# Gathered rows and activations of the experts transposed in 32x32 blocks on VectorE

## The chip, the cores and the metric

The kernel runs on one core of a Trainium2 chip, as one program. The metric is the device time in microseconds (us) of one execution, lower is better. In the rows PE is TensorE's matmuls and PEld its weight loads, DVE is VectorE, ACT is ScalarE, POOL is GpSimd, and SP is the engine that only issues the loads from memory.

## The reference

One transformer layer over 512 tokens of width 1024: attention and Fourier mixing first, then a mixture of experts, which is where the change lies. All of it is in float32.

```python
def moe(h, ...):                          # h: 512 tokens x 1024
    logits = h @ w_router + b_router
    top_logit, top_idx = lax.top_k(logits, 4)      # 4 of 32 experts for each token
    gates = jax.nn.softmax(top_logit, axis=-1)
    ...                                   # tokens sorted by expert, xb: the tokens of expert e
    g = jnp.minimum(xb @ w_gate[e] + b_gate[e], 7.0)
    u = jnp.clip(xb @ w_up[e] + b_up[e], -7.0, 7.0)
    act = g * jax.nn.sigmoid(1.702 * g) * (u + 1)
    y = act @ w_down[e] + b_down[e]       # 1024 x 1024 weights, three for each expert
    ...                                   # y times gate, added up by token
```

## The kernel before

**Units and kinds.** An expert is one unit of work, 32 in all. Their order is by the number of tokens that chose them, and the place in that order gives each unit a kind, which fixes how many token slots it has: `h` 128 slots (4 units), `m` 96 (13 units, two of them the experts 0 and 1 that come first), `l` 64 (10) and `t` 32 (5). After the first two units they go in 15 pairs, an `m` or `h` with an `l` or `t`: ten pairs m+l, four h+t (the 4th, 8th, 12th and 15th) and, first of all, one m+t. Within a pair the three matrices (`g` gate, `u` up, `d` down) alternate: m g, l g, m u, l u, m d, l d.

**Weights.** A matrix is 1024 x 1024 float32 and comes as four pieces of 1024 KB (`load_piece`, line 978, issued by SP) into a ring of 11 slots. A piece holds two of the eight blocks of 128 input features (k). SP issues a piece as soon as the products of the piece 11 places earlier have left its slot, so SP waits for PE there.

**Products.** `step_mm` makes the products of one k: the activations are the stationary operand and the weights move. PE's columns are used in tiles of 32 or 64 so that several products of few tokens run beside each other: for `m` twelve products of 32 tokens x 256 outputs for each k, for `l` two of 64 x 512, for `t` four of 32 x 256. A float32 product is two matmul instructions in the trace. `h` goes another way: weights and activations are each split into two float32r numbers, and VectorE makes the small part of the weights (`wsplit`, one 128x1024 subtraction for each k).

**Rows in, rows out.** For the product g the stationary operand must have input features on the partitions. The normalised tokens stand in a DRAM buffer (`hx2_d`, written by `post_h`, line 1141) and a unit's tokens are gathered from it: `places` and `table` (DVE) make one-hot rows, `gather` (line 1289) turns them into indices by four small products 128x4, and an indirect DMA (line 1302, POOL) brings the rows, tokens on partitions. `x_trans` (line 1328) then turns them: PE transposes of 128x128 into a PSUM bank, four to a group (two for `t`), and an ACT copy out of PSUM. The activation between u and d (`glu_g`, `glu_u`) has tokens on partitions too, and `a_trans` (line 1441) turns it in the same way. The first unit's x is not turned: `pick` makes it otherwise.

**What sets the order.** It is written out by hand: `emit_mat` emits the eight k of a matrix, and after each k `side_step` runs one step (up to the next `yield`) of at most two waiting side tasks. So `x_trans`, `a_trans`, the fetch of later units (`fetch_of`) and the scatter are spread between the products, one step for each k. `x_of(u+2)` is begun in unit u's matrix d and needed at matrix g of unit u+2, `fetch_of(u+4)` follows it. For unit 1 things are closer: its gather is in matrix g of unit 0, its `x_trans` in matrix u of unit 0, and matrix g of unit 1 is next. Engines run their instructions in order.

Of the kernel before, what the change touches and what calls it, by code (L numbers as in the profile page):

```python
# [36 lines left out]
D = 1024  # L37
# [125 lines left out]
def dit_block(ctx: ExitStack, tc: tile.TileContext, x, c, cctx, c_ctx, w_mod, b_mod, n_ap, n_ao, n_fp, n_fo,  # L163
# [712 lines left out]
    def chain(*gs):  # L876
        for g in gs:
            yield from g
# [262 lines left out]
    def post_h(t):  # L1141

        h, b = (hx[t] if t < 2 else hw[t - 2]).f, s2.f[:, 4 * t + 1:4 * t + 2]
        z = V.scalar_tensor_tensor(h, xr[t].f, b, PRE2, op0=OP.mult, op1=OP.mult)
        if t > 1:
            tc.keep_in_program_order(z)
# [61 lines left out]
    free(vec[0], wr, *hx, *xr[:2], S1f, zb, eq)  # L1208
    more_ring(2)
    xTh, xTl = R(8, 128), R(8, 128)  # L1210
    xTm = alias(xTh, 8, 128)
# [101 lines left out]
    def fetch_of(u):  # L1313

        while fetching:
            yield
        fetching.append(u)
        places(u)
        yield
        table(u)  # L1320
        for _ in range(3):
            yield
        g = gather(u, kinds[u])
        next(g)
        fetching.remove(u)
        yield

    def x_trans(kind, xh, xl=None):
        for half in range(2 if kind in "hm" else 1):
            b = tbank()  # L1330
            n = 2 if kind == "t" else 4
            for k in range(n):
                c = (4 * half + k) * 128
                tr(ps[:, b, k * 128:k * 128 + 128], xg[kind][:, c:c + 128])
            src = ps[:, b, 0:n * 128].rearrange("p (k n) -> p k n", k=n)
            c4 = slice(4 * half, 4 * half + 4)
            if kind == "h":
                split_late(xh.r[:, c4], xl.r[:, c4], src)
            else:
                z = xh[:, 4 * half:4 * half + n]  # L1340
                later(lambda src=src, z=z: act(z, src, AF.Copy), [z], [src], age=0)
            yield

    def back(u, kind):
# [95 lines left out]

    def a_trans(kind):
        a = glu_tiles(kind)[1]
        for half in range(2 if kind in "hm" else 1):
            b = tbank()
            n = min(4, WIDTH[kind] // 128 - 4 * half)
            for k in range(n):
                c = (4 * half + k) * 128
                tr(ps[:, b, k * 128:k * 128 + 128], a[:, c:c + 128])
            src = ps[:, b, 0:n * 128].rearrange("p (k n) -> p k n", k=n)
            c4 = slice(4 * half, 4 * half + 4)  # L1450
            if kind == "h":
                split_late(aTh.r[:, c4], aTl.r[:, c4], src)
            else:
                z = (aTm if kind == "m" else aTf.f)[:, 4 * half:4 * half + n]
                later(lambda src=src, z=z: act(z, src, AF.Copy), [z], [src], age=0)
            yield

    def glu_g(kind, b):
        t_, u_ = glu_tiles(kind)
# [78 lines left out]
    def step_mm(kind, mat, b, k, w, hi, lo, sel, xs):  # L1538

        first = k == 0  # L1540
        if kind == "h":
# [6 lines left out]
            for st, mv, last in ((xh, hi, False), (xh, lo, False), (xl, hi, k == 7)):  # L1548
                for h in range(2):
                    mm(ps[:, b + h], st.r[:, k], mv.r[:, h * 512:h * 512 + 512], start=first, stop=last)  # L1550
                first = False
        elif kind == "m":
# [8 lines left out]
            both = ps[96:128, b].rearrange("p (r n) -> p r n", r=2)  # L1561
            if first:
                bias = biasP.b[0:96, MAT.get(mat, 0)]
                if mat != "d":
                    for p in range(3):
                        mm(out_(0, p, 2), sel.to_broadcast([96, 32]), bias[:, 0:512], start=True, stop=False)
                else:
                    sel = selb.b[0:96, NS + 2:NS + 3]
                mm(both, sel.to_broadcast([96, 32]), bias[:, None, 768:D].to_broadcast([96, 2, 256]), start=True,
                   stop=False)  # L1570
                if mat != "d":
                    for p in range(4):
                        q = unit(2, p)[1]
                        mm(out_(2, p), sel.to_broadcast([96, 32]), bias[:, q * 256:q * 256 + 256], start=True, stop=False)
            for r in range(3):
                for p in range(4):
                    g, q = unit(r, p)
                    n = 1
                    if mat != "d":
                        st = xs[:, k, 32 * g:32 * g + 32]  # L1580
                    else:
                        fq, c = k // 2, k % 2
                        st = xs[:, 2 * fq + c, 32 * g:32 * g + 32] if fq < 3 else xs[:, 2 * g + c, 96:128]
                        if first and p < 3 and r < 2:
                            if r:
                                continue
                            n = 2
                    mm(out_(r, p, n), st, w[:, q * 256:q * 256 + 256 * n],
                       start=first and mat == "d" and (p < 3 or r == 2), stop=k == 7 and r > 0)
        else:  # L1590
            v, n = (64, 512) if kind == "l" else (32, 256)
            a, c = k // (n // 128), k % (n // 128)
            st = xs[:, c, v * a:v * a + v]
            if first and mat != "d":
                for h in range(128 // v):
                    mm(ps[v * h:v * h + v, b, 0:n], sel.to_broadcast([96, v]),
                       biasP.b[0:96, MAT[mat], h * n:h * n + n], start=True, stop=False)
                first = False
            for h in range(128 // v):
                mm(ps[v * h:v * h + v, b, 0:n], st, w[:, h * n:h * n + n], start=first, stop=k == 7)  # L1600

    def sel_of(u):
        kind, e, r = units[u]
# [69 lines left out]
    for i, (u, m) in enumerate(order):  # L1673
        kind = kinds[u]
        if i:
# [2 lines left out]
            if was == "g":  # L1678
                add(glu_g(pk, pb), True)
            elif was == "u":  # L1680
                acted[pu] = add(chain(glu_u(pk, pb, {"h": 2, "m": 2, "l": 3, "t": 5}[kind]), a_trans(pk)), True)
            else:
                finish(summed)
                y_out(pu, pk, pb)
# [36 lines left out]
        elif i == 1:  # L1721
# [5 lines left out]
            aTm = alias(aTh, 6, 128)  # L1727
            yh, yl = R(D), R(D)
            acc = [W(D) for _ in range(4)]

# [3 lines left out]
        elif i == 4:  # L1734
            settle()
            free(xT1)
            bd, gT, g3 = R(D), R(512), W(4, 96)
            xTf = W(4, 128)
        elif i == 6:
            while side and side[0] is not ready[3]:  # L1740
                finish(side.pop(0))
            settle()
            free(bd, g3, gT)
            aTf, u1l, yz = W(4, 128), W(512), R(D)

    while side:
        finish(side.pop(0))
# [136 lines left out]
```

## Time and profile before

| what | value |
|---|---|
| three timed runs | 1412.1, 1416.8, 1417.2 us, median 1416.8 |
| profiled execution, own time | 1413.2 us |
| its span, first to last instruction | 1411.4 us |
| PE busy | 1345.5 us, 95% of the span |
| DVE busy | 719.9 us, 51% |
| ACT busy | 409.3 us, 29% |
| bytes moved by DMA | 468.86 MB, mean 332 GB/s |

The first 340 us are attention and routing, the experts' products go from there to about 1387 us, and 24 us of sums and output follow. Busy time of PE says only that some matmul was under way: its instructions overlap, and their ends are modelled. Distances between the starts of following rows say more.

### The profile page before, as it was taken

To read this page: it belongs to the slowest core of one execution; us is meant where nothing else is said; L and a number is where in the kernel's file an instruction comes from. 1 tells how busy PE (TensorE), PEld (TensorE's weight loads), DVE (VectorE), ACT (ScalarE), POOL (GpSimd) and SP (SyncE) were. 2 spreads that over 40 slices of the span, in tenths; PEclk is the share of its full clock that TensorE was granted. 3 is DMA by queue.
4 is the path that set the end of the run, shared out by engine and by line. 5 is a ranking of instruction groups with operands and counts; after the bars stand their busy time and mean duration, and the time that the engine had idled before them with its cause. 6 is when DMAs were issued, how large, how long until landed. Compare 5 with 4: busy or idle time off the path is not lost. (4 is left out here: it accounts for less than half of the span.)

```text
span 1411.4 us, 30490 instructions
## 1 busy us (share of the span) xinstructions
PE 1345.5 (95%) x12966; PEld 798.2 (57%) x12967; DVE 719.9 (51%) x1329; ACT 409.3 (29%) x634; POOL 121.8 (9%) x90
## 2 busy tenths in 40 slices
PE   5998999998999999999999999999999999999993
PEld 3766887877554545466444454654544466444572
DVE  4676777755452424268423335762324287232575
ACT  5565455632110101035110103421111154010352
POOL 4355000013000000000000000000000000000002
PEclk8999999999998999999999999999999999999997
DMA  9865003667887999999999999999999999999993
GB/s 343 306 229 189 1 0 106 216 228 313 315 295 298 408 397 408 379 409 392 405 409 379 409 374 409 396 408 406 393 384 385 401 395 408 402 408 375 408 380 122
DMA packets 126496, 468.86 MB, mean 332 GB/s; under 512 B 10976, under 2 KB 12316, under 8 KB 126356
## 3 DMA queue, kind: packets, MB, share of 16 engines
q1 hardware_dynamic: 121540, 454.44, 83.2%
q0 software_dynamic: 4816, 12.43, 2.3%
q8 instruction: 103, 1.69, 0.5%
q14 instruction: 37, 0.30, 0.1%
HBM read 464.05 MB, written 6.31 MB: 333 GB/s over the span
## 5 line engine op out<-in xcount | busy, mean ns | idle before, releaser
L266 PE MATMUL ps<-s,s 128*32 128x256 f32 (+11 forms) x5364 | 892.4, 417 | 28.7 <-DMA s<-in_w_mod_dram 8.4
L266 PEld LDWEIGHTS ps<-s,s 128*128 128x128 f32 (+4 forms) x5033 | 510.8, 155 | 315.2 <-issue 182.2
L266 PE MATMUL ps<-s,a 128*32 128x256 f32 (+1 forms) x7026 | 412.7, 383 | 0.0
L266 PEld LDWEIGHTS ps<-s,a 128*32 128x32 f32 x7026 | 216.7, 110 | 158.5 <-issue 18.9
L274 ACT ACTIVATE s<-s 128x1024 fp32r<-128x1024 f32 (+8 forms) x196 | 175.9, 927 | 361.7 <-DVE s L283 308.4
L278 DVE TENSOR_TENSOR s<-s,s 128x1024 fp32r<-128x1024 f32 (+11 forms) x316 | 208.4, 686 | 32.3 <-ACT s L274 28.6
L274 ACT ACTIVATE s<-ps 128x512 fp32r<-128x512 f32 (+5 forms) x168 | 91.3, 553 | 246.0 <-PE ps L266 127.1
L278 DVE TENSOR_TENSOR s<-s,ps 128x512 f32<-128x512 f32 (+1 forms) x129 | 86.5, 682 | 82.1 <-PE ps L266 81.7
L285 DVE TENSOR_SCALAR s<-ps 128x768 f32<-128x768 f32 (+3 forms) x32 | 26.3, 823 | 185.1 <-PE ps L266 185.1
L270 PE MATMUL ps<-s,s 128*128 128x128 f32 x575 | 96.6, 288 | 15.3 <-DVE s L283 9.9
L1302 POOL DMA_INDIRECT s<-hx_d,s x31 | 32.4, 1045 | 893.3 <-PE ps L266 613.2
L270 PEld LDWEIGHTS ps<-s,s 128*128 128x128 f32 x575 | 66.4, 143 | 73.7 <-issue 45.8
L293 DVE COPY s<-ps 128x4 f32<-128x4 f32 (+5 forms) x66 | 23.7, 359 | 141.0 <-PE ps L266 117.0
L274 ACT ACTIVATE a<-ps 128x512 f32<-128x512 f32 (+1 forms) x48 | 25.9, 540 | 219.0 <-PE ps L270 219.0
L278 POOL TENSOR_TENSOR s<-s,s 128x1024 f32<-128x1024 f32 (+1 forms) x23 | 53.7, 2339 | 272.9 <-DVE s L278 211.4
L289 DVE SCALAR_TENSOR_TENSOR s<-ps,s,s 32x256 fp32r<-32x256 f32 (+5 forms) x64 | 46.2, 721 | 58.0 <-ACT s L274 52.0
L274 ACT ACTIVATE s<-ps,s 32x256 fp32r<-32x256 f32 (+7 forms) x68 | 44.8, 669 | 97.9 <-PE ps L266 90.5
L297 DVE TENSOR_TENSOR s<-ps,s 128x512 fp32r<-128x512 f32 (+1 forms) x92 | 60.6, 667 | 22.9 <-ACT s L274 22.8
L283 DVE TENSOR_SCALAR s<-ps 128x768 f32<-128x768 f32 (+4 forms) x33 | 26.5, 803 | 77.6 <-PE ps L266 77.5
L274 ACT ACTIVATE s<-s,s 128x1 f32<-128x1 f32 (+4 forms) x70 | 43.2, 644 | 13.8 <-DVE s L289 7.7
L297 DVE TENSOR_TENSOR s<-s,s 128x192 fp32r<-128x192 f32 (+5 forms) x32 | 36.0, 1144 | 8.5 <-ACT s L274 8.5
L289 DVE SCALAR_TENSOR_TENSOR s<-s,s,s 128x512 fp32r<-128x512 f32 (+5 forms) x48 | 36.8, 796 | 5.9 <-ACT s L274 4.6
(77 smaller groups left out, 289.4 us busy)
## 6 DMA issues: line engine op xcount, KB each, us to landing
s<-in_w_gate_dram SPq DMA_DIRECT2D x128, 1024.0 KB, 10.9
s<-in_w_up_dram SPq DMA_DIRECT2D x128, 1024.0 KB, 10.8
s<-in_w_down_dram SPq DMA_DIRECT2D x128, 1024.0 KB, 7.9
s<-in_w_mod_dram SPq DMA_DIRECT2D x32, 512.0 KB, 4.6
s<-in_w_mod_dram SPq DMA_DIRECT2D x8, 1024.0 KB, 16.3
s<-in_x_dram SPq DMA_DIRECT2D x8, 512.0 KB, 8.3
s<-in_w_out_dram SPq DMA_DIRECT2D x8, 512.0 KB, 5.1
s<-in_w_in_dram SPq DMA_DIRECT2D x1, 2560.0 KB
```

Of the source, the lines that this page charges most:

```text
L266: pin(nc.tensor.matmul(o, a, b, start=start, stop=stop))
L270: pin(nc.tensor.transpose(o, i, ident))
L274: return nc.scalar.activation(o, i, f, **kw)
L278: return eng.tensor_tensor(o, a, b, op=op)
L283: eng.tensor_scalar(o, a, s1, s2, op0=op0)
L285: eng.tensor_scalar(o, a, s1, s2, op0=op0, op1=op1)
L289: V.scalar_tensor_tensor(o, a, s, b, op0=op0, op1=op1)
L293: eng.tensor_copy(o, i)
L297: later(lambda: eng.tensor_tensor(lo, src, hi, op=OP.subtract), [lo], [src, hi])
L1302: nc.gpsimd.indirect_dma_start(out=xg[kind], out_offset=None, in_=src, in_offset=bass.IndirectOffsetOnAxis(ap=idxs.i[:, u:u + 1], axis=0), ...
```

## The change

The transposes on PE and the copies out of PSUM go, except those of `a_trans` for kind `h`. In their place VectorE transposes blocks of 32x32 from one SBUF tile into another. One such instruction turns eight blocks that lie side by side, so it takes 32 partitions x 256 columns (or 128 x 256 where all four quarters can go at once). A block that is turned stays at the place of its own row of blocks, so feature 128b + 32q + r of a token has to stand at column 256q + 32b + r of the row: `post_h` writes `hx2_d` in that order (four instructions on DVE in place of one, and an addition on POOL over reordered views), and the products g and u of kinds m, l and t write their outputs in that order, by reading the moving weights as eight runs of 32 columns, 128 apart, in place of one run. For `l` this makes eight products of 32 x 256 for each k in place of two of 64 x 512. `h` gets an ACT copy and a DVE subtraction of 128x1024 for its split. A step of `x_trans` is two instructions. Three more steps lie between table and gather (6, not 3), and `glu_u` is followed by `a_trans` at once for all kinds but h.

```diff
 def post_h(t):
-        z = V.scalar_tensor_tensor(h, xr[t].f, b, PRE2, op0=OP.mult, op1=OP.mult)
-        tt(h, h, SH2, op=OP.add, eng=nc.gpsimd)
+        hv = h.rearrange("p (q b r) -> p b q r", q=4, r=32)
+        xv, pv, sv = (v.rearrange("p (b q r) -> p b q r", q=4, r=32) for v in (xr[t].f, PRE2, SH2))
+        for q in range(4):
+            z = V.scalar_tensor_tensor(hv[:, :, q], xv[:, :, q], b, pv[:, :, q], op0=OP.mult, op1=OP.mult)
+        tt(hv, hv, sv, op=OP.add, eng=nc.gpsimd)
...
+    ROWS = {"h": 128, "m": 96, "l": 64, "t": 32}
...
         table(u)
-        for _ in range(3):
+        for _ in range(6):
             yield
         g = gather(u, kinds[u])
...
 def x_trans(kind, xh, xl=None):
-        for half in range(2 if kind in "hm" else 1):
-            b = tbank()
-            n = 2 if kind == "t" else 4
-            for k in range(n):
-                c = (4 * half + k) * 128
-                tr(ps[:, b, k * 128:k * 128 + 128], xg[kind][:, c:c + 128])
-            src = ps[:, b, 0:n * 128].rearrange("p (k n) -> p k n", k=n)
...
+        if kind in "lt":
+            w, g = SLOTS[kind], xg[kind]
+            for s in range(w // 32):
...
+                for n, (o, i_) in enumerate(turns):
+                    i_ = i_.rearrange("p (b r) -> p b r", r=32)
+                    guard([o], [i_])
+                    V.transpose(o, i_)
+                    if n % 2 or kind == "t":
+                        yield
+            return
+        z = xg[kind].rearrange("p (q b r) -> p q b r", q=4, r=32)
+        for s in range(ROWS[kind] // 32):
+            rw = slice(32 * s, 32 * s + 32)
+            for q in range(4):
+                o = (xTw if kind == "h" else xh)[32 * q:32 * q + 32, :, rw]
+                guard([o], [z[rw, q]])
+                V.transpose(o, z[rw, q])
+                if q % 2 and (kind == "m" or q == 3):
+                    yield
+        if kind == "h":
+            act(xh.r, xTw, AF.Copy)
+            later(lambda: tt(xl.r, xTw, xh.r, op=OP.subtract), [xl.r], [xTw, xh.r], age=0)
             yield
...
 def a_trans(kind):
...
+        for s in range(ROWS[kind] // 32):
+            o = (aTm if kind == "m" else aTf.f)[:, :, 32 * s:32 * s + 32]
+            i_ = a[:, 256 * s:256 * s + 256].rearrange("p (b r) -> p b r", r=32)
+            guard([o], [i_])
+            V.transpose(o, i_)
+        yield
...
 def step_mm(kind, mat, b, k, w, hi, lo, sel, xs):
+        elif mat != "d":
+            n = ROWS[kind] // 32
+            def cols(z, q):
+                return z.rearrange("p (b q r) -> p q b r", q=4, r=32)[:, q]
+            def tile_(q, s, n=1):
+                return ps[32 * q:32 * q + 32, b + s // 2, 256 * (s % 2):256 * (s % 2) + 256 * n]
...
+            for s in range(n):
+                for q in range(4):
+                    mm(tile_(q, s), xs[:, k, 32 * s:32 * s + 32], cols(w, q), start=False,
+                       stop=k == 7 and (s % 2 == 1 or s + 1 == n))
```

On PE, in a later pair (matrix m d of the second pair), the rows before were these; `s_2561` and `s_2569` are ring slots, `a_3014` the turned activation of `m`, `s_2733` the gathered rows, `s_3748` the activation of `l`, `s_67` the identity:

```order
L266 MATMUL ps<-s_2561,a_3014 32x512 x3
L266 MATMUL ps<-s_2561,a_3014 32x256 x6
L270 MATMUL ps<-s_67,s_2733 128x128 x4
L266 MATMUL ps<-s_2561,a_3014 32x256 x12
L270 MATMUL ps<-s_67,s_2733 128x128 x4
L266 MATMUL ps<-s_2569,a_3014 32x256 x12
L270 MATMUL ps<-s_67,s_3748 128x128 x4
```

Now the same matrix has nothing between its products (`a_3029` is the turned activation):

```order
L266 MATMUL ps<-s_2561,a_3029 32x512 x3
L266 MATMUL ps<-s_2561,a_3029 32x256 x18
L266 MATMUL ps<-s_2569,a_3029 32x256 x24
L266 MATMUL ps<-s_2577,a_3029 32x256 x24
L266 MATMUL ps<-s_2585,a_3029 32x256 x24
```

Three groups of four transposes have left that matrix, and on DVE it now has these rows, where `s_2746` is the gathered rows of the next `m`, `a_2711` its turned x, and `s_3741` and `s_3740` the activation of `l` before and after:

```order
L285 TENSOR_SCALAR s_3741<-ps 128x512
L289 SCALAR_TENSOR_TENSOR s_3741<-s_3741,s_3740 128x512
L1480 STREAM_TRANSPOSE s_3740<-s_3741 128x8x32 x2
L1358 STREAM_TRANSPOSE a_2711<-s_2746 32x8x32 x12
L278 TENSOR_TENSOR s_2737<-s_2335,s_2745 128x128
```

The two clamping steps of `glu_u` stood there before too; behind them DVE has fourteen more instructions, and the fetch of a later unit comes after those.

On PE at the beginning of the experts, matrix u of unit 0, the rows before were these; `a_2699` is unit 0's x, `s_2733` the gathered rows of unit 1, and unit 1's gather (128x4 products) had been in matrix g:

```order
L266 MATMUL ps<-s_2341,a_2699 32x256 x24
L266 MATMUL ps<-s_2343,a_2699 32x256 x24
L270 MATMUL ps<-s_67,s_2733 128x128 x4
L266 MATMUL ps<-s_2537,a_2699 32x256 x12
L270 MATMUL ps<-s_67,s_2733 128x128 x4
L266 MATMUL ps<-s_2537,a_2699 32x256 x12
```

Now (unit 0's x is `a_2711`) the gather stands in that matrix, ahead of the counts of tokens (128x32):

```order
L266 MATMUL ps<-s_2341,a_2711 32x256 x24
L266 MATMUL ps<-s_2326,s_2731 128x4 x4
L266 MATMUL ps<-s_2343,a_2711 32x256 x12
L266 LDWEIGHTS s_2323
L266 MATMUL ps<-s_2350,s_2323 128x32
```

It moved back by three k. On DVE the transposes of unit 1 (`s_2871` is its turned x) now come behind the work on the routing, with one 128x960 comparison between them, and unit 0's clamping steps (`s_2870`) come behind all twelve:

```order
L283 TENSOR_SCALAR s_2597<-s_2595,s_2142 128x30
L1358 STREAM_TRANSPOSE s_2871<-s_2746 32x8x32 x2
L278 TENSOR_TENSOR s_2745<-s_2595,s_2142 128x960
L1358 STREAM_TRANSPOSE s_2871<-s_2746 32x8x32 x10
L285 TENSOR_SCALAR s_2870<-ps 128x768
L289 SCALAR_TENSOR_TENSOR s_2870<-s_2870,s_2869 128x768
L1480 STREAM_TRANSPOSE a_3029<-s_2870 128x8x32 x3
```

These three rows of transposes are new, and matrix g of unit 1 waits for the first two.

## Rows read from the trace of the kernel before

**Rows 1.** The page: engines' busy us, share of the span, instructions.
```profile
PE 1345.5 (95%) x12966; PEld 798.2 (57%) x12967; DVE 719.9 (51%) x1329; ACT 409.3 (29%) x634; POOL 121.8 (9%) x90
```
**Rows 2.** Waits of SP's queue: total us, times, longest us.
```profile
SPq L978 <- PE ps L266: 728.5, 323, 21.3
```
**Rows 3.** Waits of PE from 400 to 1380 us, same columns.
```profile
PE ps L266 <- DVE s L278: 6.8, 8, 1.8
PE ps L266 <- DVE s L283: 4.5, 5, 2.9
```
**Rows 4.** Windows: length, busy us (PE, PEld, DVE, ACT, POOL), PE clock, DMA share, GB/s.
```profile
820.00:840.00 20.00, 20.00 (x216) 9.26 (x219) 7.22 (x10) 1.47 (x2) 0.00 (x0) 1.00 0.94 347
840.00:860.00 20.00, 20.00 (x231) 8.94 (x227) 4.65 (x8) 1.61 (x4) 0.00 (x0) 1.00 1.02 410
433.50:447.20 13.70, 12.87 (x60) 6.20 (x64) 6.18 (x10) 0.00 (x0) 0.00 (x0) 0.50 0.51 196
460.00:1375.00 915.00, 905.82 (x9218) 475.94 (x9207) 415.45 (x751) 207.35 (x294) 27.29 (x26) 1.00 1.01 397
```
**Rows 5.** Windows: four pairs between the gathers of the larger units (first, last and sum).
```profile
543.50:609.60 66.10, 66.10 (x743) 31.34 (x743) 23.07 (x49) 8.10 (x14) 1.99 (x3) 1.00 1.00 393
609.60:670.20 60.60, 60.08 (x373) 39.99 (x369) 49.70 (x73) 30.95 (x38) 2.48 (x3) 1.00 1.01 399
...
sum 259.60, PE 257.43 PEld 133.85 DVE 116.21 ACT 55.40 POOL 8.42; mean PE 64.36 PEld 33.46 DVE 29.05 ACT 13.85 POOL 2.11
```
**Rows 6.** The page: DMA issues with KB of one and us to landing.
```profile
s<-in_w_gate_dram SPq DMA_DIRECT2D x128, 1024.0 KB, 10.9
```
**Rows 7.** The page: POOL's DMA queue: packets, MB, share of 16 engines' span.
```profile
q0 software_dynamic: 4816, 12.43, 2.3%
```
**Rows 8.** Timeline of PE in one pair: start us, us, instruction and count.
```profile
724.93 0.66 PE L270 MATMUL ps<-s,s 128*128 128x128 f32 x4
725.52 1.50 PE L266 MATMUL ps<-s,a 128*32 128x256 f32 x24
726.95 0.66 PE L270 MATMUL ps<-s,s 128*128 128x128 f32 x4
...
729.56 5.39 PE L266 MATMUL ps<-s,a 128*32 128x256 f32 x96
734.88 0.61 PE L266 MATMUL ps<-s,s 128*128 128x4 f32 x4
```
**Rows 9.** Groups of DVE by form, 460 to 1375 us: count, busy us, mean ns.
```profile
L278 DVE TENSOR_TENSOR s<-s,s 128x128 f32<-128x128 f32 x52 | 14.9, 287 | 0.9
L278 DVE TENSOR_TENSOR s<-s,s 128x768 f32<-128x768 f32 x10 | 9.6, 958 | 9.1 <-ACT s L274 9.1
L293 DVE COPY s<-ps 32x256 f32<-32x256 f32 x11 | 4.7, 426 | 13.3 <-ACT s L274 13.3
```
**Rows 10.** Window: matrices h d and t d of a pair h+t.
```profile
654.40:674.90 20.50, 19.24 (x142) 13.12 (x138) 17.04 (x32) 11.01 (x14) 0.99 (x1) 1.00 1.03 408
```
**Rows 11.** Groups of PE by form, whole span: products of 128x256 over all columns.
```profile
L266 PE MATMUL ps<-s,s 128*128 128x256 f32 x336 | 55.9, 291 | 1.4 <-DVE s L297 0.7 <-ACT s L839 0.4 <-DVE s L293 0.3
```
**Rows 12.** Timeline around matrix u of unit 0.
```profile
347.87 0.61 PE L266 MATMUL ps<-s,s 128*128 128x4 f32 x4
349.98 1.09 POOL L1302 DMA_INDIRECT s<-hx_d,s  x1 [10.55 <-DVE s L278]
362.17 1.16 PE L266 MATMUL ps<-s,s 96*32 96x512 bf16 x20
```
**Rows 13.** The gather of unit 1: us from issue to landing.
```profile
DMA to landing us min/median/max: 4.3/4.3/4.3
```
**Rows 14.** Timeline of the end: SP's last loads, PE's last rows.
```profile
1349.28 15.23 SPq L978 DMA_DIRECT2D s<-in_w_down_dram  x8
1387.47 2.05 PE L266 MATMUL ps<-s,s 64*128 64x512 f32 x9 [0.30 <-DVE s L289]
```
**Rows 15.** Groups of DVE by form, 300 to 340 us: `post_h` of one tile.
```profile
L1144 DVE SCALAR_TENSOR_TENSOR s<-s,s,s 128x1024 f32<-128x1024 f32 x4 | 5.0, 1278 | 2.2 <-PE ps L266 2.2
```

More of the change, by code (lines that the diff above doesn't have):

```diff
@@ L1442, in a_trans @@
         a = glu_tiles(kind)[1]
[L1443 to L1451, printed above, removed]
-                split_late(aTh.r[:, c4], aTl.r[:, c4], src)
[L1453 to L1456, printed above, removed]
+        if kind == "h":
+            for half in range(2):
+                b = tbank()
+                for k in range(4):
+                    c = (4 * half + k) * 128
+                    tr(ps[:, b, k * 128:k * 128 + 128], a[:, c:c + 128])
+                src = ps[:, b].rearrange("p (k n) -> p k n", k=4)
+                c4 = slice(4 * half, 4 * half + 4)
+                split_late(aTh.r[:, c4], aTl.r[:, c4], src)
+                yield
+            return
+        for s in range(ROWS[kind] // 32):
[3 more added lines that the diff above has]
+            V.transpose(o, i_)
+        yield
     def glu_g(kind, b):
@@ L1551, in step_mm @@
                 first = False
+        elif mat != "d":
[4 more added lines that the diff above has]
+                return ps[32 * q:32 * q + 32, b + s // 2, 256 * (s % 2):256 * (s % 2) + 256 * n]
+            if first:
+                for s in range(0, n, 2):
+                    m = min(2, n - s)
+                    for q in range(4):
+                        z = cols(biasP.b[0:96, MAT[mat]], q)
+                        o = tile_(q, s, m)
+                        if m == 2:
+                            o = o.rearrange("p (m b r) -> p m b r", m=2, r=32)
+                            z = z[:, None].to_broadcast([96, 2, 8, 32])
+                        mm(o, sel.to_broadcast([96, 32]), z, start=True, stop=False)
+            for s in range(n):
+                for q in range(4):
+                    mm(tile_(q, s), xs[:, k, 32 * s:32 * s + 32], cols(w, q), start=False,
+                       stop=k == 7 and (s % 2 == 1 or s + 1 == n))
         elif kind == "m":
@@ L1558, in out_ @@
                 return ps[32 * p:32 * p + 32, b + r // 2, 256 * (r % 2):256 * (r % 2) + 256 * n]
-            both = ps[96:128, b].rearrange("p (r n) -> p r n", r=2)
             if first:
[L1563 to L1574, printed above, removed]
+                both = ps[96:128, b].rearrange("p (r n) -> p r n", r=2)
+                zero = selb.b[0:96, NS + 2:NS + 3].to_broadcast([96, 32])
+                mm(both, zero, biasP.b[0:96, 0][:, None, 768:D].to_broadcast([96, 2, 256]), start=True, stop=False)
             for r in range(3):
@@ L1578, in step_mm @@
                     n = 1
[L1579 to L1589, printed above, removed]
+                    if first and p < 3 and r < 2:
+                        if r:
+                            continue
+                        n = 2
+                    mm(out_(r, p, n), xs[:, k, 32 * g:32 * g + 32], w[:, q * 256:q * 256 + 256 * n],
+                       start=first and (p < 3 or r == 2), stop=k == 7 and r > 0)
         else:
             v, n = (64, 512) if kind == "l" else (32, 256)
[L1592 to L1598, printed above, removed]
             for h in range(128 // v):
-                mm(ps[v * h:v * h + v, b, 0:n], st, w[:, h * n:h * n + n], start=first, stop=k == 7)
+                mm(ps[v * h:v * h + v, b, 0:n], xs[:, k, 0:v], w[:, h * n:h * n + n], start=first, stop=k == 7)
     def sel_of(u):
@@ L1737, in dit_block @@
             bd, gT, g3 = R(D), R(512), W(4, 96)
-            xTf = W(4, 128)
+            xTf = W(8, 64)
         elif i == 6:
```

24 lines of the change are left out of this document (12 added, 12 removed).

## The prediction, made before the changed kernel ran

> **What bounds the kernel now.** I read the page first, for shares: PE is busy 95% of the span, DVE 51% [rows 1]. A busy PE need not set the end, so the waits come next. SP, which issues the weights, spends 728.5 us waiting for products to leave a ring slot, 323 times [rows 2], while PE's waits for DVE between 400 and 1380 us are a few us each, and none of its waits there for a weight piece is larger [rows 3]. So PE holds the loads up, and not the other way round. How much faster could the loads go? The windows answer: 347 GB/s in one stretch of 20 us, 410 in the next, where the share of busy DMA time is 1.02, and 397 as the mean from 460 to 1375 us [rows 4]. About 408 is therefore the ceiling, and the kernel is already near it: PE sets the pace by a small margin. That margin is what the change can win.
>
> The pattern repeats every four pairs (three m+l, one h+t): 259.6 us, with PE busy in 257.4 of them and DVE in 116.2 [rows 5].
>
> **The loads' floor.** Four pairs take 24 matrices of four pieces, 96 pieces of 1024 KB [rows 6], 100.7 MB: 246.7 us at 408 GB/s. The small transfers of POOL's queue use the same 16 engines for 2.3% of the span, 32.5 us in all [rows 7]. Some 40 transfers carry it (31 gathers, the writes of `hx_d` and `hx2_d`), about 0.8 us each, so the eight gathers of four pairs cost some 6.5 us. The floor is about 253, 6 us under the period.
>
> **What PE gives up.** A group of four transposes starts 0.59 us before the products that follow it (724.93 to 725.52). Those 24 instructions take 1.43 us to the next start, where 96 in a row take 5.32, or 1.33 for 24. So a group costs 0.59 + 0.10, about 0.7 us; a group of two I put at 0.45, between that and half of it [rows 8]. An `m` loses four groups (x 4+4, `a` 4+2), `l` two, `t` two of two, and `h` two (its `a` stays on PE): 4.0 us for m+l, some 2.3 for h+t, 14.3 in four pairs. Gone too are PE's waits for DVE's table at the gather (11.3 us in 15 pairs at most, [rows 3]; some 2 in four pairs, taken), since six k lie between now. `l` has eight products in place of two, but four run beside each other and the columns that they stream are the same; I take 0.8 in four pairs against it. PE would need 259.6 − 14.3 − 2 + 0.8 = 244. That is below the floor of 253: the loads become the bound and only some 6 of 15.5 us come back.
>
> **What DVE takes on.** The trace has no such transpose. The cheapest nearby row of about that size is 0.29 us (128x128, in place of 32x256), the dearest a 128x768 subtraction at 0.96; I take 0.43, the copy of 32x256, since it moves the same shape [rows 9]. An m+l pair has 25 of them (12 and 8 for x, 3 and 2 for `a`): 10.8 us on top of some 23 in 66 [rows 5]. That is hidden. The place to look at is matrices h d and t d, where DVE is busy 17.0 of 20.5 us [rows 10] and, going by an `m` that follows, gets 12 more (5.2 us): 2 us late. What is late then is the next table and the next activation; the pair has PE to spare (some 58 us of products against 63 of loads), so I cost it at nothing. Without that cover it is 2 us in each of four h+t pairs; at 0.96 for one it would be 9 late against a cover of 5, 4 us each.
>
> On this price the Trainium skill (VectorE: DVE Perf Modes, "The three transpose paths") gives 311 ns for 128x128 in bf16 on DVE and calls it the fastest for 32x32 blocks. An estimate from it, twice that for 256 columns, is 0.62 us: 4.8 more per m+l pair, still hidden, and the sum stays. No run so far shows it.
>
> **Weights in runs of 32 columns.** The products g and u of m, l and t now read the moving rows in eight runs. The nearest rows are those of attention's values, where 108 of 336 products of 128x256 take the moving operand in two runs of 128: the group as a whole has a mean of 291 ns [rows 11], and 24 products of 32x256 on four column tiles, 6 to a tile, need 1.33 us, 222 ns each [rows 8]. That bounds nothing from above; two runs may be too few to show it. I take nothing, and keep the dear end as a rival.
>
> **The start of the experts.** Unit 1's gather moves back three k. Before, its four products started at 347.87, POOL's DMA at 349.98, and matrix g of unit 1 at 362.17 [rows 12], with the landing 4.3 us after issue [rows 13]. A k of this `m` takes 1.33 or, while weights still arrive, up to 1.8: three put the products at 352.3, POOL at 354.4, the landing at 358.7. Then DVE makes twelve transposes and one 128x960 comparison between them, 12 × 0.43 + 1.2 (scaled from 128x768), so the last ends at about 365. Matrix g would be ready at 362 less the two groups gone, 361. A wait of 4 us, between 0 (the transposes at 0.29 and half of them enough to start) and 10 (at 0.96). Queued behind it on PE are all later products, and the ring is full, so SP waits too. A wait has a second price in this trace: after an idle PE of 2.87 us the granted clock was 0.50 for 13.7 us (1.2 of 2.4 GHz), with loads at 196 GB/s [rows 4]. Products of such a stretch done at half clock lose up to 7 us; I take 3.
>
> **The end.** SP's last eight issues run from 1349.28 to 1364.5, PE's last products start at 1387.47 [rows 14]. At 10.9 us to landing [rows 6] the last weights are there at 1375.4, and PE trails by 12. When loads are the bound it trails by about 4, the products of one piece of each unit. That gives 8.
>
> **The sum.** From 460 to 1375 there are 915 / 64.9 = 14.1 pairs: 6.1 × 14.1 / 4 = −21 (a check: 915 × 397 / 408 is 890, −25). The end −8. Transposes before 460, some nine groups while PE is the bound, −6. The wait at unit 1 +4 and its clock +3. `post_h` has four instructions for one of 1.28 us [rows 15]: 4 × 0.43 or so is +0.5 a tile, of which two lie on the path, +1. Lateness of DVE in h pairs and `l`'s products +2. Together −25: the profiled 1413.2 becomes 1388; the median of the timed runs is 3.6 above the profiled one, so **1391** for the new median.
>
> **The rivals.**
> *DVE, or the dips in the loads, keep part.* If the loads run at 400 and not 408 in the mean (the window's 347 shows that they dip for reasons other than a full ring), the floor is 258 and the steady gain 5; or, with a transpose at 0.96, the h pairs lose 16 and unit 1's wait is 10. Either way some 1402 to 1409, say 1406. For it: the 347. Against: SP's long waits for PE, which say that the dip is PE's doing.
> *No change.* The mean share of DMA is already 1.01 [rows 4]; if that means that the loads are the bound now, then what PE gives up turns into waits for weights, and the gain at the start goes into unit 1's wait: 1413 to 1419. Against: SP's waits for PE. The Trainium skill (DMA: Bandwidth & Descriptors, "Where 436 GB/s comes from") puts what one core gets from memory at about 358 GB/s, which speaks for this case; by it four pairs would take 281 us, and the trace has them in 259.6, so the trace differs.
> *Slower: PE reads strided weights more slowly.* Products g and u of m, l and t take about 110 of the 259.6 us of four pairs (8 × 1.33 for a matrix of m, some 7 for l, 3.5 for t). PE's 244 reaches the old period when they cost 14% more; from there on the kernel is slower. At 25% PE needs 244 + 27.5 = 271.8, 12.2 more per four pairs, 3.6 of these: +44, less what the end gives, about 1455. For it: no row reads such short runs. Against: 291 ns for products of which a third are in runs of 128. The Trainium skill (Advanced Engine Details and Errata, "Memory Cachelines") says that any non-contiguous access pattern in PSUM slows matmuls significantly, while in SBUF two hits on a line of 16 bytes are enough; here the writes to PSUM stay contiguous, and a run of 32 float32 has many hits, so by that page nothing is lost. No run shows it yet.
> *The change doesn't do what it says* is excluded by the order: the transposes have left PE.
>
> **Chances.** The forecast, 1378 to 1400: 0.60. Part kept back, 1400 to 1410: 0.20. No change: 0.09. Slower: 0.11. A measurement of this kernel tells about 0.5%, 7 us, from no change, so the first two are faster: 0.80, same 0.09, slower 0.11. Range 1376 (unit 1's wait, its clock and the last three us of the sum at nothing, the loads at 410: 25 + 7 + 3 + 4, some 40 in all) to 1409 (DVE at its dear bound).
>
> **What would show it.** Period of four pairs near 253 with PE waiting for pieces of weights, and SP's wait for PE far below 728 us: right on the bound. A period still near 260 with SP still waiting for PE: products are dearer; 24 of them then start more than 1.33 us apart. Transposes of 32x256 near 0.43 us. PE idle some 4 us at matrix g of unit 1, with granted clock 0.5 behind it. The last products within 5 us of the last landing. Two things above all would make the forecast wrong: strided reads at over 10%, or a transpose on DVE above 0.8 us.

## The result, and the profile after

The changed kernel takes 1402.1 us (median of seven runs, 1397.4 to 1407.4), the kernel before 1412.9 beside it (seven runs). The ratio is 0.9919 with a 95% interval of 0.9893 to 0.9945: 0.8% faster. The forecast was 25 us of gain, and 11 came. The time lies in the range, nearest to the rival in which DVE keeps part of the gain.

The page of the changed kernel: engines, the rate of the loads in 40 slices of the span (35 us each), and the transposes of x.

```profile
PE 1298.0 (93%) x14620; PEld 824.4 (59%) x14621; DVE 871.6 (62%) x1694; ACT 368.3 (26%) x550; POOL 125.3 (9%) x90
GB/s 344 305 241 187 1 1 106 220 229 310 308 309 300 409 393 408 408 409 408 351 401 408 408 407 408 408 408 377 408 407 407 408 408 409 332 407 397 408 408 134
L1358 DVE STREAM_TRANSPOSE a<-s 32x256 f32<-32x256 f32 x196 | 84.7, 432 | 2.8
```

PE is busy for 47.5 us less and DVE for 152 us more (against [rows 1]). A transpose of 32x256 takes 432 ns; the forecast had 0.43. In the experts' part the loads run at 407 to 409 GB/s in most slices; before, stretches of 20 us went from 347 to 410 [rows 4]. But three slices are low (351, 377, 332).

Now SP's queue: the first issue of each down matrix's loads marks off the pairs. First the kernel before, then the changed one (start us, us, instruction, count).

```profile
507.29 16.66 SPq L978 DMA_DIRECT2D s<-in_w_down_dram  x8
573.45 16.66 SPq L978 DMA_DIRECT2D s<-in_w_down_dram  x8
637.98 15.23 SPq L978 DMA_DIRECT2D s<-in_w_down_dram  x8
700.73 16.66 SPq L978 DMA_DIRECT2D s<-in_w_down_dram  x8
```
```profile
503.61 16.46 SPq L978 DMA_DIRECT2D s<-in_w_down_dram  x8
565.02 16.46 SPq L978 DMA_DIRECT2D s<-in_w_down_dram  x8
629.39 15.23 SPq L978 DMA_DIRECT2D s<-in_w_down_dram  x8
699.01 16.46 SPq L978 DMA_DIRECT2D s<-in_w_down_dram  x8
...
1337.03 15.23 SPq L978 DMA_DIRECT2D s<-in_w_down_dram  x8
```

The differences tell most of the story. An m+l pair went from 66.2 to 61.4 us. The interval into the h+t pair stayed (64.5 and 64.4), and the one behind it went the other way, from 62.8 to 69.6. Over the 13 pairs from the first of these rows to the last such load (before: [rows 14]) it is 842.0 before and 833.4 after. The whole account, with the load of the tokens (340.17 and 337.79) as the start of the experts:

| stage | before, us | after, us | forecast | measured |
|---|---|---|---|---|
| ahead of the experts | 340.2 | 337.8 | +1 | −2.4 |
| start, to the first down load above | 167.1 | 165.8 | +1 | −1.3 |
| 13 pairs | 842.0 | 833.4 | −18 | −8.6 |
| last loads of the down matrices and behind | 62.1 | 62.6 | −8 | +0.5 |

The forecast's −21 is for 14.1 pairs; 13 of them are −20, or −18 with its +2 for lateness and for `l`'s products. The first row is hardly a gain of the change: the changed kernel's relatives below, alike up to there, begin their experts between 336.3 and 339.8 us, and a second form of the kernel before (fewer bytes, below) at 338.0. Two terms failed: 13 pairs give 8.6 and not 18, and the end gives nothing.

What happens behind an h pair? PE's rows there, and DVE's ahead of the long wait:

```profile
656.58 1.65 PE L266 MATMUL ps<-s,s 128*128 128x512 f32 x6 [0.52 <-DVE s L278]
...
668.70 4.07 PE L266 MATMUL ps<-s,a 128*32 128x256 f32 x72
676.54 3.79 PE L266 MATMUL ps<-s,s 128*128 128x512 f32 x6 [3.76 <-DVE s L283]
680.26 2.45 PE L266 MATMUL ps<-s,a 128*32 128x256 f32 x24
682.63 2.26 PE L266 MATMUL ps<-s,s 128*128 128x512 f32 x6
...
688.86 1.50 PE L266 MATMUL ps<-s,a 128*32 128x256 f32 x24
690.29 2.25 PE L266 MATMUL ps<-s,s 128*128 128x512 f32 x6
```
```profile
656.56 0.88 DVE L1358 STREAM_TRANSPOSE a<-s 32x256 f32<-32x256 f32 x2
657.47 1.23 DVE L278 TENSOR_TENSOR s<-s,s 128x1024 fp32r<-128x1024 f32 x1
...
667.35 3.57 DVE L1348 STREAM_TRANSPOSE s<-s 32x256 f32<-32x256 f32 x8
...
673.92 1.97 DVE L289 SCALAR_TENSOR_TENSOR s<-ps,s,s 32x256 fp32r<-32x256 f32 x4
675.90 0.88 DVE L283 TENSOR_SCALAR s<-s,s 128x512 fp32r<-128x512 f32 x2
```

In h d each k has two transposes of the next m (0.88) ahead of the subtraction that splits the next weights (1.23), together 2.1 us, where PE needs 1.65: it waits 1.34 us at the first such k and 0.5 at each of the next four, 3.4 us in all. In t d the eight transposes of the next l stand in a row, then table work, then the outputs of t and the scatter's one-hot rows, for which PE waits 3.76 us. Behind that wait 24 products start 2.37 us apart from the next (680.26 to 682.63), and later 1.43 (688.86 to 690.29). The windows there, and behind the last of these waits (columns as in [rows 4]):

```profile
660.00:680.00 20.00, 15.22 (x166) 8.25 (x164) 16.74 (x41) 2.98 (x5) 1.39 (x1) 0.88 1.03 408
680.00:700.00 20.00, 20.00 (x235) 10.18 (x238) 7.46 (x14) 0.84 (x1) 1.00 (x1) 0.94 0.82 307
1180.00:1200.00 20.00, 16.21 (x142) 7.54 (x145) 11.60 (x31) 1.86 (x4) 1.39 (x1) 0.68 1.03 407
1200.00:1220.00 20.00, 20.00 (x288) 10.86 (x284) 6.89 (x14) 1.47 (x2) 1.00 (x1) 0.97 0.73 275
```

The reader is to see the order: PE waits (15 of 20 us busy) and its clock falls, while the loads still run at 408; 20 us later PE is busy throughout and the loads are at 307 and 275 GB/s. I read this as the ring having filled, so that what PE lost is now taken from the loads.

### The profile page after: what moved, and what is told of

It is laid out like the page before. It is cut to its first block, busy times and chain, and to the rows that moved or that the text cites. A ratio compares the mean times of both kernels' runs of the same rounds, so it can differ in the third digit from the quotient of the medians.

```text
span 1399.6 us, 34033 instructions
## 1 busy us (share of the span) xinstructions
PE 1298.0 (93%) x14620; PEld 824.4 (59%) x14621; DVE 871.6 (62%) x1694; ACT 368.3 (26%) x550; POOL 125.3 (9%) x90
## 5 line engine op out<-in xcount | busy, mean ns | idle before, releaser
L266 PE MATMUL ps<-s,s 128*32 128x256 f32 (+6 forms) x7324 | 887.7, 388 | 63.0 <-DVE s L283 21.2
L266 PEld LDWEIGHTS ps<-s,s 128*32 128x32 f32 (+3 forms) x6953 | 549.4, 140 | 340.4 <-issue 123.0
L266 PE MATMUL ps<-s,a 128*32 128x256 f32 (+1 forms) x7026 | 408.6, 386 | 0.0
L266 PEld LDWEIGHTS ps<-s,a 128*32 128x32 f32 x7026 | 233.8, 111 | 156.2 <-issue 18.9
L274 ACT ACTIVATE s<-ps 128x512 fp32r<-128x512 f32 (+4 forms) x128 | 69.8, 557 | 305.3 <-PE ps L266 246.6
L1307 POOL DMA_INDIRECT s<-hx_d,s x31 | 36.3, 1172 | 894.4 <-DVE s L278 849.0
L1358 DVE STREAM_TRANSPOSE a<-s 32x256 f32<-32x256 f32 x196 | 84.7, 432 | 2.8
L297 DVE TENSOR_TENSOR s<-ps,s 128x512 fp32r<-128x512 f32 (+1 forms) x84 | 55.0, 665 | 16.3 <-ACT s L274 16.2
L270 PE MATMUL ps<-s,s 128*128 128x128 f32 (+1 forms) x269 | 44.3, 289 | 16.6 <-DVE s L283 10.0
L270 PEld LDWEIGHTS ps<-s,s 128*128 128x128 f32 (+1 forms) x269 | 33.7, 147 | 30.0 <-DVE s L283 10.0
## 6 DMA issues: line engine op xcount, KB each, us to landing
s<-in_w_gate_dram SPq DMA_DIRECT2D x128, 1024.0 KB, 13.7
s<-in_w_down_dram SPq DMA_DIRECT2D x128, 1024.0 KB, 10.9
```

What stands on the lines that cost most here:

```text
L266: pin(nc.tensor.matmul(o, a, b, start=start, stop=stop))
L270: pin(nc.tensor.transpose(o, i, ident))
L274: return nc.scalar.activation(o, i, f, **kw)
L297: later(lambda: eng.tensor_tensor(lo, src, hi, op=OP.subtract), [lo], [src, hi])
L1307: nc.gpsimd.indirect_dma_start(out=xg[kind], out_offset=None, in_=src, in_offset=bass.IndirectOffsetOnAxis(ap=idxs.i[:, u:u + 1], axis=0), ...
L1358: V.transpose(o, z[rw, q])
```

## The experiments

The theory (1): DVE's transposes in h d and t d make PE wait, and what follows the wait is the loss. The rivals are named where they are tested. For each kernel "13 pairs" is the same stage as in the table, read from its one profiled execution; the times are medians of four to ten runs.

**The twelve transposes of the m behind an h.** Two kernels take them off DVE. The first only copies:

```diff
+        if u >= 2 and kinds[u - 2] == "h":
+            return x_copy(src)
+    def x_copy(xh):
+        act(xh, xg["m"].rearrange("p (k n) -> p k n", k=8), AF.Copy)
```

> The changed kernel, but the x of the m that follows each h is not turned: one ACT copy of the gathered rows stands in place of the twelve transposes on DVE in matrices h d and t d (that x is then wrong). Theory 1 (those transposes stand on DVE between the subtractions that the products of h wait for, DVE sets the pace there, PE waits, its clock falls and the ring stays full): the pairs after the three inner h+t pairs, 69.6, 68.6 and 72.4 us between loads of the down matrix, fall to 62 to 64, and the time from 1402 to about 1382. Rival 2 (PE waits there because weights are short everywhere now): these pairs stay at 69 to 72 and the time within 3 us of 1402.

Measured: 1394.2 us, ratio to before 0.9881 (0.9848 to 0.9914). The pairs behind h+t are 65.9, 65.8 and 70.4 us, 13 pairs 824.8. The second makes the same x on PE:

```diff
+                for q in range(4):
+                    mm(ps[32 * q:32 * q + 32, b, k * 128:k * 128 + 128], v[:, q, 4 * half + k], ident, start=True, stop=True)
+            later(lambda src=src, z=z: act(z, src, AF.Copy), [z], [src], age=0)
```

> The changed kernel, but the x of the m that follows each h is turned on PE: 32 products of 32 columns of rows with the identity into PSUM and two ACT copies, in place of twelve transposes on DVE. All is computed. Theory 1: PE has about 1 us more in each of four places and DVE 5.2 us less, so the three pairs go to 63 to 65 us and the time to about 1384. Rival 2: no gain, 1402 to 1406.

Measured: 1393.5 us, 0.9868 (0.9842 to 0.9895); the pairs 67.2, 65.8 and 65.8, 13 pairs 821.6 (its profiled execution was the slowest of the six, 1399.8 us, with 176.6 us from the start to the first of these loads). The direction is theory 1's and against rival 2, but each gives 8 us where 18 to 20 were expected: these transposes are a part of the cause.

**Three blocks in place of six**, the change's own part undone (`range(3)` in `fetch_of`).

> The changed kernel with three steps between table and gather as before, in place of six. Theory 1: the loss behind the h pairs is DVE's work and stays; PE waits for the table again where the gather comes early (up to 11 us in 15 pairs, but hidden where the loads are the bound), and the wait of 2.65 us at matrix g of the second unit goes: 1399 to 1406. Rival 3 (six steps make rows and turned x late behind an h, and that is the loss): the three pairs go back to 63 us and the time to about 1382.

Measured: 1399.0 us, 0.9903 (0.9875 to 0.993), not to be told from the changed kernel. The pairs behind h+t stay at 70.5 to 70.7, so rival 3 falls. Underneath, two things cancel: 13 pairs take 840.2 (833.4 with six blocks), and the start to the first of those loads 159.3 (165.8). Six blocks are worth 7 us in the pairs, and cost 6.5 at the beginning.

**Each transpose twice**, to see what DVE's time is worth.

```diff
                 V.transpose(o, z[rw, q])
+                V.transpose(o, z[rw, q])
```

> The changed kernel with each transpose on DVE made twice, one after the other. Theory 1: an m+l pair, where DVE goes from some 34 to 45 of 61 us, stays at 61.4 us; the stretch from h d to the scatter behind it gets 20 x 0.43 = 8.6 us more DVE, and the 16 of an h ahead of it 7 more, so the time goes to 1430 to 1445. Rival 2: DVE is nowhere the bound, 1400 to 1408.

Measured: 1570.6 us, 1.1127 (1.1091 to 1.1162), 168 us more than the changed kernel and not 28 to 43. Rival 2 falls, and with it the expectation that an m+l pair would hide even twice as many: it goes from 61.4 to 72.6 us. PE's wait at the scatter of such a pair, and DVE over the stage:

```profile
590.36 2.90 PE L266 MATMUL ps<-s,s 96*128 96x512 f32 x6 [8.40 <-DVE s L283]
460.00:1335.00 875.00, 746.75 (x9063) 426.83 (x9055) 573.19 (x1171) 134.37 (x174) 26.28 (x22) 0.91 0.89 345
```

DVE is busy 66% there. Its share says that there is room; but 40 transposes in two rows (24 and 16) stand ahead of the scatter's operands, and PE waits 8.40 us for those.

**The l behind a t one matrix later**, in the next g, where nothing waits for DVE.

```diff
+            if kind == "t":
+                held[u + 2] = x_
+            else:
+                ready[u + 2] = add(x_)
+        if m == "g" and u + 1 in held:
+            ready[u + 1] = add(held.pop(u + 1))
```

> The changed kernel, but the x of the l that follows each t (and the fetch behind it) begins one matrix later, in the next matrix g, not in t d. All is computed. Theory 1, second part (matrix t d is short, and in it DVE has eight transposes in a row, the next table and t's outputs, so that the first product of the scatter waits 3.65 us for DVE and PE's clock is at half behind it): this wait, five times, falls below 1 us, the granted clock stays up there, the pairs after h+t go from 69 to 72 down to 64 to 66, and the time to about 1388. Rival 4 (what PE waits for there is the twelve transposes of the m in h d alone): no change there, 1400.

Measured: 1393.8 us, 0.9887 (0.9865 to 0.991), 13 pairs 823.8. The first scatter behind a t, before and after this edit:

```profile
480.65 3.62 PE L266 MATMUL ps<-s,s 96*128 96x512 f32 x6 [3.65 <-DVE s L283]
```
```profile
480.83 0.71 PE L266 MATMUL ps<-s,s 96*128 96x512 f32 x2 [0.42 <-DVE s L283]
```

The wait is gone (0.42), and pairs behind h+t are 64.5, 66.4 and 66.6, against rival 4. The time is 6 us above the expectation.

**Both repairs**, and then the second unit's gather early as well (`range(3 if u == 1 else 6)`).

> Both repairs: x of the m after each h on PE, x of the l after each t one matrix later. All is computed. Theory 1: no wait for DVE over 1.5 us is left behind the h pairs, half clock only in the first 110 us of the experts, the pairs after h+t at 62 to 64 and the time 1380 to 1385. Rival 2: as without the second repair, 1393.

> As the kernel with both repairs, and the second unit's gather comes after three steps, as before the change; all later ones after six. Theory 1: the wait of 2.65 us at matrix g of that unit goes, 2 to 6 us less than with both repairs, about 1378. Rival 5 (the front is bound by the half clock behind other waits, so nothing of it comes back): the same time as with both repairs.

Measured: 1390.4 us, 0.9856 (0.9831 to 0.9881), and 1383.9, 0.9825 (0.9802 to 0.9848). Both are 5 to 6 us slower than expected. With both repairs 13 pairs take 826.2 us, and the pairs behind h+t are 62.2, 67.9 and 66.4, not 62 to 64. The early gather shortens the start from 163.3 to 155.3 us in the profiles. In the last of them the loads' rate over the stage, PE's waits for weights, and the first and last loads of the 13 pairs:

```profile
460.00:1335.00 875.00, 851.61 (x10885) 495.65 (x10877) 518.44 (x1007) 165.96 (x215) 29.46 (x26) 0.99 1.02 406
PE ps L266 <- DMA s<-in_w_down_dram: 1.9, 5, 0.6
493.12 16.46 SPq L978 DMA_DIRECT2D s<-in_w_down_dram  x8
...
1317.97 19.51 SPq L978 DMA_DIRECT2D s<-in_w_down_dram  x8
```

406 GB/s, where the same window has 398 before and 400 in the changed kernel: PE now waits for weights, if briefly (and 7.2 us for ACT, which prepares the weights of an `h` and itself waits for their landing). 13 pairs are 824.9 us.

**Filler products.** Does the wait cost the time, or the clock behind it? This kernel leaves DVE late and gives PE four products to throw away while it waits.

```diff
+                if t == h == 0 and kinds[us[-1]] == "t":
+                    for _ in range(4):
+                        mm(ps[:, b], ident, toks.f, start=True, stop=True)
```

> The changed kernel, with four more products (128x512, their sums thrown away) on PE ahead of the first product of each scatter behind a t, where PE waits 3.65 us for DVE. They leave DVE's lateness as it is and fill the wait. Theory 6 (most of the loss there is what comes after the wait: the granted clock falls to 0.5, PE falls behind, the ring stays full and the loads dip to 275 to 353 GB/s): the clock stays at 1.0 behind these waits, the pairs after h+t go from 69 to 72 down to 65 to 66, and the time to about 1390 to 1393. Rival 7 (the wait itself is the loss, 3.65 us in each of four or five places, and the clock only goes with it): the same pairs and the same time, 1399 to 1404, or 2 to 3 us more for each place where the fillers outlast the wait.

Measured: 1389.9 us, 0.9834 (0.9821 to 0.9848): 12 us faster than the changed kernel, by adding work to its busiest engine. 13 pairs 824.1. The same four windows as above, and the first and last loads:

```profile
660.00:680.00 20.00, 19.35 (x199) 9.73 (x198) 16.19 (x40) 2.98 (x5) 1.39 (x1) 1.00 1.03 408
680.00:700.00 20.00, 20.00 (x290) 11.02 (x293) 7.44 (x15) 1.47 (x2) 1.00 (x1) 1.00 1.00 380
1180.00:1200.00 20.00, 19.86 (x172) 9.44 (x174) 10.15 (x21) 0.00 (x0) 2.39 (x2) 1.00 1.00 397
1200.00:1220.00 20.00, 20.00 (x380) 12.08 (x372) 5.42 (x9) 1.47 (x2) 0.00 (x0) 1.00 1.00 387
501.72 16.46 SPq L978 DMA_DIRECT2D s<-in_w_down_dram  x8
...
1325.81 18.76 SPq L978 DMA_DIRECT2D s<-in_w_down_dram  x8
```

The clock is 1.00 in all four and the loads hold 380 to 408. PE cannot go on with real products any sooner than before, so rival 7 falls: the clock at half (1.2 of 2.4 GHz) behind the wait was the loss. The pairs behind h+t went to 67.1 each, a little above what was expected, from 69.6, 68.6 and 72.4; that is the whole difference of the 13 pairs (9.3 us).

The changed kernel's own trace agrees. Its three waits there are alike (3.76, 3.77 and 3.79 us), but the half clock behind them isn't equally long. The second of them, and the windows around it:

```profile
933.35 2.67 PE L266 MATMUL ps<-s,s 128*128 128x512 f32 x6 [3.77 <-DVE s L283]
920.00:940.00 20.00, 16.23 (x187) 8.37 (x187) 14.68 (x39) 2.98 (x5) 1.39 (x1) 0.91 1.03 408
940.00:960.00 20.00, 20.00 (x287) 10.96 (x289) 7.49 (x15) 1.48 (x2) 1.00 (x1) 1.00 0.93 353
```

The clock that is missing in each two windows (1 less the mean, times 20 us) is 3.6, 1.8 and 7.0 us; the pairs lie 2.5, 1.5 and 5.3 us above 67.1. For one and the same wait, the more clock is missing, the longer the pair.

**Fewer bytes**, in the kernel with all repairs and in the kernel before.

```diff
+        n = D if i < NX + NRING else 896
+        nc.sync.dma_start(slot.f[:, :, 0:n], ...[:, 2 * h:2 * h + 2, 0:n])
```

> The kernel with both repairs and the early gather of the second unit, but each piece of weights behind the first 16 is loaded only up to column 896 of 1024 (the rest of a slot keeps older weights, so the outputs are wrong). 12.5% fewer bytes. Theory 8 (the loads are the bound there: 824.9 us for 13 pairs, 63.4 each, is what 408 GB/s allow): the pairs fall to what PE and DVE need, 59 to 61, and the time by 25 to 45 us, to 1340 to 1360. Rival 9 (PE or DVE is still the bound and the loads only just keep up): within 6 us of 1384.

> The kernel before, with the same 12.5% fewer bytes for pieces behind the first 16 (outputs wrong). Theory 8 (before, PE is the bound): an m+l pair stays at 66.2 us and the time moves by less than 10 us. Rival 10 (the loads were the bound before as well): pairs fall by several us and the time by over 30.

Measured: 1370.6 us, 0.9707 (0.9692 to 0.9722) for the repaired one, 13 us faster than with all bytes; 1412.0, 0.9996 (0.9983 to 1.0009) for the kernel before. Their first and last loads of the stage:

```profile
495.18 16.46 SPq L979 DMA_DIRECT2D s<-in_w_down_dram  x8
...
1304.79 15.23 SPq L979 DMA_DIRECT2D s<-in_w_down_dram  x8
```
```profile
505.16 16.66 SPq L979 DMA_DIRECT2D s<-in_w_down_dram  x8
...
1347.12 15.25 SPq L979 DMA_DIRECT2D s<-in_w_down_dram  x8
```

Before, 13 pairs take 842.0 us with an eighth of the bytes gone, and 842.0 with all: PE is the bound and the loads follow, as the prediction read it. Repaired, they take 809.6 and 824.9: the loads are the bound, but with little below them. Theory 8 holds; its size (25 to 45 us) does not.

**Fillers at the front**, on top of the repairs (condition `us == (1,)`), and fillers at both places with the early gather alone, DVE's work left as the change has it.

> The kernel with both repairs and the early gather, and four filler products ahead of the first product of the second unit's scatter, where PE waits 2.50 us for DVE and its clock is at half behind. Theory 6 (half clock behind a wait is lost time where PE is the bound, as it is in the first 110 us of the experts): the clock stays at 1.0 there, and the time falls by 3 to 6 us, to 1378 to 1381. Rival 7 (the wait itself is what counts): 1383 to 1385.

> The changed kernel with the early gather of the second unit and the fillers alone (ahead of the scatters behind a t and of the second unit's), DVE's work left where the change put it. Theory 6: the wait at the scatter is covered and no clock falls behind it, so it comes within 5 us of the kernel with both repairs and the early gather: 1380 to 1387. Rival 7: DVE's lateness needs its own repair, and without it 1392 or more.

Measured: 1381.3 us, 0.9786 (0.977 to 0.9802), and 1382.6, 0.9795 (0.9782 to 0.9808). The front's window without and with the filler:

```profile
424.00:444.00 20.00, 17.50 (x192) 9.33 (x196) 9.04 (x19) 2.10 (x5) 1.20 (x1) 0.83 0.81 297
```
```profile
424.00:444.00 20.00, 20.00 (x237) 10.71 (x233) 8.87 (x19) 2.46 (x5) 1.19 (x1) 1.00 0.91 336
```

The clock no longer falls there. The first kernel gains some 3 us, at the edge of what was expected and of what these runs can tell. The second says more: with DVE as late as in the changed kernel, 13 pairs take 824.1 us, the same as with every repair. Both beat the kernel before by 2%, and the changed one by some 1.3% (0.9786 and 0.9795 against 0.9919).

## Why the prediction was right or wrong

**What bounds the kernel: right.** PE before (842.0 us with and without an eighth of the bytes). The loads' floor, 253 us in four pairs or 63.3 each, stands too: 824.9 / 13 is 63.4 in the repaired kernel, where PE waits for weights and fewer bytes give 809.6. Six of the eight kernels with repairs or fillers take 823.8 to 824.9, the other two 821.6 and 826.2. In the two with fillers and no repair PE shows no wait for weights: their four pairs of 61.4, 61.4, 64.4 and 67.1 us make 254.3, just above the floor.

**Strided weights: right.** 192 products of unit 0's first matrix, all in runs of 32 columns, start 10.72 us ahead of what follows, 1.34 for a k (forecast 1.33). The rival of slower products falls.

```profile
336.76 10.97 PE L266 MATMUL ps<-s,a 128*32 128x256 f32 x192
347.48 0.58 PE L266 MATMUL ps<-s,s 96*32 96x512 bf16 x8
```

The rule on SBUF in the Trainium skill (Advanced Engine Details and Errata, "Memory Cachelines") asks for two hits on a line of 16 bytes; runs of 128 bytes that cost nothing agree with it.

**The price of a transpose: right.** 432 ns for 32x256, near 0.43. The estimate from the Trainium skill (VectorE: DVE Perf Modes, "The three transpose paths") was 0.62 us; the measurement decides, and is below it.

**PE's new need: mis-sized.** The sum had 244 us in four pairs. With fewer bytes the repaired kernel takes 809.6 / 13 × 4 = 249.1, so the bound under the loads is 5 us higher (that kernel still turns one x in four pairs on PE). The m+l pairs are at 61.4 in both, so they gave a little more than forecast (4.8 against 4.0 and the table's waits). The h stretch gave next to nothing: 64.4 and 62.3 there, 64.5 and 62.8 before (2.3 forecast).

**The step that failed.** It is "the pair has PE to spare ..., so I cost it at nothing", said of DVE's lateness in h d and t d. (The sum has +2 for it and `l`'s products together.) Its kind was right, its size was not: the forecast counted the twelve transposes of the next `m` and left out the eight of the next `l`, which stand in t d (3.57 us in the rows above). It had DVE 2 us late; PE waits 3.4 us in h d and 3.76 at the scatter. With the wait filled such a pair takes 67.1 us, with the work moved away and fewer bytes 62.2: 4.9 us, about all of the room that the loads leave (253 against 249.1 in four pairs). So it still hides, but only just: the fillers leave it in place, and the 13 pairs come to 824.1. What was left out altogether is the second price, which the prediction did count, but only for unit 1: half clock behind the wait. It came behind the scatters of a `t`, and the loads lost there what PE could not free: 833.4 − 824.1, about 9 us. That is what the 13 pairs fell short by (18 forecast, 8.6 measured).

**The start: near, in part by luck.** The forecast was −6 for the transposes, +4 for the wait and +3 for its clock, +1 in all, and −1.3 was measured. No row takes the −6 apart. The wait is 0.30 + 1.17 + 1.18 = 2.65 us, split over the first three groups of products:

```profile
360.06 0.64 PE L266 MATMUL ps<-s,s 128*32 128x256 f32 x8 [0.30 <-DVE s L1358]
361.88 0.64 PE L266 MATMUL ps<-s,s 128*32 128x256 f32 x8 [1.17 <-DVE s L1358]
363.69 10.56 PE L266 MATMUL ps<-s,s 128*32 128x256 f32 x181 [1.18 <-DVE s L1358]
```

In this execution the clock stayed at 1.00 behind it (359 to 376 us), so its +3 is not in the profiled run: that is the luck. In the kernel with both repairs the same wait (2.75 us) was followed by half clock (0.83 in the mean of 360 to 370 us), and the same 181 products took longer:

```profile
364.34 12.25 PE L266 MATMUL ps<-s,s 128*32 128x256 f32 x181 [1.18 <-DVE s L1358]
```

The early gather took 8 us off the start of that kernel. Matrix g of unit 1 with the bias products ahead of it lasts 16.4 us there (359.81 to 376.20) and 11.3 with the early gather (359.00 to 370.33): 2.75 of wait and 2.3 of clock, where the forecast had 4 and 3. The other 2.9 us lie behind the wait of 2.5 us at unit 1's scatter, which both kernels have: the 72 products there start 13.7 us ahead of what follows in the first (mean clock 0.52) and 10.8 in the second (0.68). So they can't be put down to the gather.

**The end: wrong.** I took 8 us because PE would trail the last landing by 4 and no longer by 12. In the changed kernel the last piece, issued at about 1352 us, takes 13.7 to land, and PE's last products start some 10 us behind that. (The 10.9 us to landing in the sum are those of the gate's pieces; the page of the kernel before has 7.9 for the down matrices.) The stretch from the last down loads is 62 to 64 us in every kernel here but two (66.3 with the l later alone, 61.4 for the repaired one with fewer bytes): its last pair is an h+t, and its last products start 38.6 us behind the first of these loads (1337.03 to 1375.65), 38.2 before. That the h pair's PE and DVE pace this end fits, but no run took it apart.

**The rivals.** The one that part is kept back came, at 1402 where it had 1406, and by a third way: neither dear transposes nor dips of the loads' own, but the clock. That the time lies in the stated range is luck in so far as its upper end stood for a DVE at its dear bound, which did not come. (In the rival of slower products 244 + 27.5 is 271.5, not 271.8, which changes nothing.) My test of "loads are the bound", SP's wait for PE far below 728, failed in the changed kernel, which has 683.6:

```profile
SPq L978 <- PE ps L266: 683.6, 321, 21.3
```

Even the repaired kernel has 612.3: SP issues one piece behind the next with a full ring, so it waits for PE even where the loads are the bound, which is how I read the number. The rate of the loads is the better sign.

## What to carry to other kernels

A busy share is no room for work on an engine that runs in order: ask what stands behind the new instructions and who waits for that (DVE at 66% made PE wait 8.4 us at one scatter). Price a wait of TensorE twice, once for its length and once for the granted clock behind it, and look for the second in the windows after the wait, where the loads dip. Where a wait can't be moved, products that nobody needs can fill it, and they are worth a trial before DVE's order is rebuilt.

## What the runs showed of the hardware that was not expected

Four products that are thrown away, 12 us faster: the granted clock fell to 0.88 and 0.68 (mean of 20 us) where PE had waited 3.8 us, and stayed at 1.00 where the same wait was filled. Like waits did not cost alike: the pairs of three waits of 3.8 us in one execution were 2.5, 1.5 and 5.3 us longer than with the wait filled. An eighth of the bytes of each piece behind the first 16 can go from a kernel that moves 397 GB/s of some 408 without changing its time by more than a measurement can tell (0.9996), since PE was the bound by that small margin.
